# Hybrid encoder layer: block sums' transfers begun from GpSimd, and a delta-rule scan in which the state meets the keys themselves

## The chip, the cores and the metric

One core of a Trainium2 chip. The metric is the device time of one execution in microseconds, the median of several runs. Engines by name: TensorE (PE), VectorE (DVE), ScalarE (ACT), GpSimd (POOL) and SyncE (SP), which only issues DMA transfers here.

## What is computed

One encoder layer on 1024 tokens of width 1024, all in float32. Three mixers run side by side on a projection of the normalised input: a gated delta rule in both directions (4 heads of 128, chunks of 64), attention of 8 heads, and cross-attention of 4 heads into 256 memory tokens. Their outputs are gated and merged; an MLP of width 4096 with squared ReLU follows (`w_up`, `w_down`). The delta rule, cut to what the change touches (one direction, one chunk at a time):

```python
rhs = jnp.concatenate([vb, kb * jnp.exp(gc)[..., None]], axis=-1)
sol = lax.linalg.triangular_solve(lmat, rhs, left_side=True, lower=True, unit_diagonal=True)
u, w = sol[..., :dv], sol[..., dv:]
...
def step(state, inp):
    u_i, w_i, q_i, k_i, a_i, gl = inp
    v_new = u_i - jnp.einsum("bhcd,bhdv->bhcv", w_i, state)
    o = jnp.einsum("bhcd,bhdv->bhcv", q_i, state) + jnp.einsum("bhcs,bhsv->bhcv", a_i, v_new)
    state = state * jnp.exp(gl)[..., None, None] + jnp.einsum("bhcd,bhcv->bhdv", k_i, v_new)
    return state, o
```

With T the inverse of the triangular matrix (beta folded in), u = T·v and w = T·(k·exp(gc)), so v_new = T·v − (T·(k·exp(gc)))·S = T·(v − exp(gc)·(k·S)).

## The kernel before

The layer runs in stages. In the order of the trace: projection, convolution and preparation of keys and queries to about 445 us; the delta-rule scan, 448 to 571 us; the attention stage, 588 to 1018 us; the branch stage with the gated merge, from 1018 us; then the output projection, the MLP's first gemm, and from about 1650 us the second one, by `w_down`.

Large gemms split each float32 operand into a high and a low part (`split`, L138 to L140) and take three products. `ld` (L97) issues a transfer from SP. Tiles come from pools with a few buffers, and an instruction that writes a buffer waits for the last reader of what was in it. Each engine, and each queue, works in the order of its instructions. That order comes from a scheduler that simulates a timeline, except that TensorE's in the attention stage is pinned to the program's.

**The scan** (loop at L870 to L883) has 16 steps. A step takes two chunks at once, one of the forward and one of the backward direction, in the two halves f of the 128 partitions, for 4 heads. `scan_pre(n)` prepares step n and is written ahead of the step before. It loads `tf`/`Tr` (the inverse T), `kn` (keys), `vn` (values), `wq` (queries in the slots 1 and 2 of four) and `Ar`; it transposes half of T (`ca,tf` on TensorE) and copies it (L790). Then `vn·Tr` gives T·v, which ACT copies to `u` (L797). GpSimd makes `ke` (L792) and multiplies `kn` by `eg` = exp(gc) (L799); `Tr·kn` gives w, transposed, and ACT copies it into the slots 0 and 3 of `wq` (L803). `scan_main(n)` is the part that needs the state `St`: `wq·St` (two PSUM tiles `ps_sm`, 4 heads each, which hold both w·S and q·S in different halves), VectorE's subtraction from `u` (L817, one for each half), `ke·u` (8 products), VectorE's update of `St` (L829, 8 operations), ACT's scaling of q·S into `o` (L833, 8 operations), `ar·u`, and the sum into `oacc` (L841). In the second half of the steps `dn_out` (L846) normalises and stores finished chunks, on VectorE, ACT, GpSimd and TensorE.

**The attention stage** (loop at L1043) has 64 steps t. In each, TensorE does the scores of step t + 2, the transposes of step t, and in between pieces of the gate projection and of `cross()`. `cross()` loads keys and values of a head of the cross-attention into `mkv`, a tile with one buffer, four transfers, once for each of 4 heads; so a head's load waits for the products of the head before.

**Block sums.** Each step t also calls `block_sums(t // 4, t % 4)` (L1024 to L1032), 64 calls. One call loads two pieces of `w_down` into a tile `wc` (2 transfers of 128 KB), makes four differences on GpSimd (L1031) and stores the 256 KB tile to `wt_d` in HBM, which only the last gemm reads. The pool of `wc` has 2 buffers; a load into one waits for the store of what was there. All these transfers are issued by SP through `ld`, in one queue with all other loads of the stage (`qh`, `cxq`, `mkv`, `w_raw`) and stores.

Of the kernel before, what the change touches and what calls it, by code (L numbers as in the profile page):

```python
# [9 lines left out]
F32 = mybir.dt.float32  # L10
F32R = mybir.dt.float32r
AF = mybir.ActivationFunctionType
ALU = mybir.AluOpType
# [6 lines left out]
P = 128  # L20
# [43 lines left out]
def bc(ap, axis, n):  # L64
    a = ap.unsqueeze(axis)
    shape = list(a.shape)
    shape[axis] = n
    return a.broadcast_to(shape)
# [18 lines left out]
def hybrid_block(tc, x, mem, mix_norm_w, w_in, dn_conv_w, dn_a_log, dn_dt_bias, dn_norm_w, q_norm_w, k_norm_w,  # L87
                 mem_norm_w, w_mem_kv, w_branch, w_out, ffn_norm_w, w_up, w_down, final_norm_w, ca_d, cb_d, rope_d,
                 out, dbg=None):
    nc = tc.nc  # L90
    pe, act, dve, gp = TensorE(tc), nc.scalar, nc.vector, nc.gpsimd
    def ld(out, in_):
        if out.dtype == F32R:
            out = out.bitcast(F32)
        if in_.dtype == F32R:
            in_ = in_.bitcast(F32)
        return nc.sync.dma_start(out=out, in_=in_)  # L97
# [4 lines left out]
    def pool(st, name, bufs=1, space=None, side=None):  # L102
        kw = {}
        if space is not None:
            kw["space"] = space
        if side is not None:
            kw["side"] = side
        if space is not DRAM:
            kw["reuse_waits"] = "tile"
        return st.enter_context(tc.tile_pool(name=name, bufs=bufs, **kw))  # L110
# [70 lines left out]
    kT_d = dram.tile([8, P, 4, P], F32, name="kT_d")  # L181
# [16 lines left out]
    wt_d = [dram.tile([P, 4, 512], F32, name=f"wt_d{k}") for k in range(16)]  # L198
# [5 lines left out]
    def ps_mm():  # L204
        return pmm.tile([P, 512], F32, name="ps_mm", tag="mm")

    def ps_dn():
        return pp.tile([P, 512], F32, name="ps_dn", tag="dn", bufs=4)
# [22 lines left out]
    eg = cor.tile([P, 2, 8, 4], F32, name="eg")  # L231
# [25 lines left out]
    for c in range(0, D, 512):  # L257
        ps = ps_mm()
# [9 lines left out]
    for m in range(8):  # L268
# [3 lines left out]
        for g in range(2):  # L272
            ps = ps_dn()
# [17 lines left out]
    R = [slice(0, 64), slice(64, 128)]  # L291
# [147 lines left out]
    for h in range(4):  # L439
# [20 lines left out]
        for m in range(8):  # L460
            for f in range(2):
                pe.matmul(psq[f * 64:(f + 1) * 64, 2 * m:2 * m + 2], lhsT=sq[:, m * P + (1 - f) * 64:m * P + (2 - f) * 64],
                          rhs=ones, start=True, stop=True)
# [268 lines left out]
    for j in range(1, 63):  # L732
        n = 63 - j
# [18 lines left out]
    dp = pool(dst, "dp", bufs=2, side="right")  # L752
# [7 lines left out]
    def f4(a):  # L760
        return a.rearrange("p h c -> p (h c)")

    def nps():
        return ps1b.tile([P, 512], F32, name="ps_sm", tag="sm", bufs=4)

    def nps2():
        return ps1b.tile([P, 512], F32, name="ps_sp", tag="sp", bufs=2)

    def scan_pre(n):
        y = 0 if n < 8 else 1  # L770
        m = n if y == 0 else 15 - n
        a = y
        b = 1 - a
        tr, ar = Tr[n % 2], Ar[n % 2]
        ys = slice(y * 4, y * 4 + 4)
        tf = dp.tile([P, 4, 64], F32, name="tf", tag="tf")
        ld(out=tf[R[a]], in_=ts_d[m, a, ys].rearrange("h r c -> r h c"))
        ld(out=tr[R[b], :, R[b]], in_=ts_d[m, b, ys].rearrange("h r c -> r h c"))
        kn = dp.tile([P, 4, P], F32, name="kn", tag="kn")
        vn = dp.tile([P, 4, P], F32, name="vn", tag="vn")  # L780
        wq = dp.tile([P, 4, 4, 64], F32, name="wq", tag="wq")
        ld(out=kn, in_=kn_d[m])
        ld(out=vn, in_=vn_d[m])
        ld(out=wq[:, :, 1:3], in_=qT_d[m].rearrange("p h (f c) -> p h f c", f=2))
        for f in range(2):
            ld(out=ar[R[f], :, R[1 - f]], in_=at_d[m][R[f], ys])
        ps = nps2()
        for h in range(4):
            pe.matmul(ps[R[a], h * 64:(h + 1) * 64], lhsT=tf[R[a], h], rhs=ident[R[a], R[a]], start=True, stop=True)
        act.copy(out=tr[R[a], :, R[a]], in_=ps[R[a], :256].rearrange("p (h c) -> p h c", h=4))  # L790
        ke = dp.tile([P, 4, P], F32, name="ke", tag="ke")
        gp.tensor_tensor(out=ke, in0=kn, in1=bc(kd[:, y, m], 2, P), op=ALU.mult)  # L792
        u = dp.tile([P, 4, P], F32, name="u", tag="u")
        ps = nps2()
        for h in range(4):
            pe.matmul(ps[:, h * P:(h + 1) * P], lhsT=tr[:, h], rhs=vn[:, h], start=True, stop=True)
        act.copy(out=f4(u), in_=ps)  # L797
        if n > 0:
            gp.tensor_tensor(out=kn, in0=kn, in1=bc(eg[:, y, m], 2, P), op=ALU.mult)  # L799
            ps = nps2()  # L800
            for h in range(4):
                pe.matmul(ps[:, h * P:(h + 1) * P], lhsT=kn[:, h], rhs=tr[:, h], start=True, stop=True)
            act.copy(out=wq[:, :, 0::3], in_=ps.rearrange("p (h f c) -> p h f c", h=4, f=2))  # L803
        return y, m, [y, 1 - y], ar, ke, u, wq

    def scan_main(n, pre):
        y, m, pair, ar, ke, u, wq = pre
        o = dp.tile([P, 4, P], F32, name="o", tag="o")
        pss = []
        if n > 0:  # L810
            for f in range(2):
                ps = nps()
                pss.append(ps)
                for h in range(4):
                    pe.matmul(ps[:, h * P:(h + 1) * P], lhsT=wq[:, h, 2 * f:2 * f + 2].rearrange("p f c -> p (f c)"),
                              rhs=St[pair[f]][:, h], start=True, stop=True)
                dve.tensor_tensor(out=f4(u)[R[f]], in0=f4(u)[R[f]], in1=ps[R[f]], op=ALU.subtract)  # L817
        if n < 15:
            psk = [nps(), nps()]
            for h in range(4):  # L820
                for f in range(2):
                    pe.matmul(psk[f][:, h * P:(h + 1) * P], lhsT=ke[R[f], h], rhs=u[R[f], h], start=True, stop=True)
        for f in range(2 if n < 15 else 0):
            s, ps = St[pair[f]], psk[f]
            if n == 0:
                act.copy(out=f4(s), in_=ps)
            else:
                for h in range(4):
                    dve.scalar_tensor_tensor(out=s[:, h], in0=s[:, h], scalar=el[f][:, y, m, h:h + 1],  # L829
                                             in1=ps[:, h * P:(h + 1) * P], op0=ALU.mult, op1=ALU.add)  # L830
        for f, ps in enumerate(pss):
            for h in range(4):
                act.activation(out=o[R[1 - f], h], in_=ps[R[1 - f], h * P:(h + 1) * P], func=AF.Copy,  # L833
                               scale=egs[R[1 - f], y, m, h:h + 1])
        ps = nps()
        for h in range(4):
            scan_end[0] = pe.matmul(ps[:, h * P:(h + 1) * P], lhsT=ar[:, h], rhs=u[:, h], start=True, stop=True)
        if n == 0:
            act.copy(out=f4(oacc[m]), in_=ps)
        elif y == 0:  # L840
            dve.tensor_tensor(out=f4(oacc[m]), in0=f4(o), in1=ps, op=ALU.add)  # L841
        else:
            dve.tensor_tensor(out=f4(o), in0=f4(o), in1=ps, op=ALU.add)
            gp.tensor_tensor(out=oacc[m], in0=oacc[m], in1=o, op=ALU.add)
# [24 lines left out]

    scan_end = [None]  # L870
    pre = scan_pre(0)
    for n in range(16):
        nxt = scan_pre(n + 1) if n < 15 else None
        scan_main(n, pre)
        pre = nxt
        if n == 4:
            tc.keep_in_program_order(ld(out=kA, in_=ka_d))
        if n == 5:
            tc.keep_in_program_order(ld(out=kB, in_=kb_d))
        if n > 9:  # L880
            dn_out(17 - n)
# [142 lines left out]
    def block_sums(k, c):  # L1024
        cs = slice(c * P, (c + 1) * P)
        w = wcp.tile([P, 4, P], F32, name="wc", tag="wc")
        for j in range(2):
            src = w_down[(2 * k + j) * P:(2 * k + j + 1) * P].rearrange("p (h c) -> p h c", h=2)
            ld(out=w[:, 2 * j:2 * j + 2], in_=src[:, :, cs])
        for o, a, b in ((0, 1, 0), (1, 3, 1), (3, 3, 0), (2, 2, 3)):  # L1030
            gp.tensor_tensor(out=w[:, o], in0=w[:, a], in1=w[:, b], op=ALU.subtract)  # L1031
        ld(out=wt_d[k][:, :, cs], in_=w)  # L1032

    cr = cross()
    fill(24 * GATES[0])
# [7 lines left out]
    for t in range(NT):  # L1043
        if t + 2 < NT:
            q_scores(t + 2)
        if t % 2 == 0 and t:
            q_out(t // 2 - 1)
        next(cr, None)
        fill(FILL[0])
        q_trans(t, 0)  # L1050
        block_sums(t // 4, t % 4)
        fill(FILL[1])
        q_trans(t, 1)
        fill(FILL[2])
# [19 lines left out]
    def ps2():  # L1074
        return pq.tile([P, 512], F32, name="ps2", tag="ps2")
# [11 lines left out]
    for bi, b in enumerate(order):  # L1087
# [7 lines left out]
        for mt in range(8):  # L1095
# [11 lines left out]
            for f in range(2):  # L1107
                c = slice(f * 512, (f + 1) * 512)
# [35 lines left out]
    for m in range(8):  # L1144
# [5 lines left out]
        for f in range(2):  # L1150
            c = slice(f * 512, (f + 1) * 512)
            ps = ps2()
# [192 lines left out]
    for name in ("P1", "P2", "P6", "P7", "P4", "P5", "P3"):  # L1345
        ps = [ps2() if m < 3 else ps_mm() for m in range(4)]
        for kg in range(16 // KG):
# [9 lines left out]
            for m in range(4):  # L1357
# [7 lines left out]
                u, o1, o2 = us[m], o[m], o[m + 4]  # L1365
# [61 lines left out]
```

## Time and profile before

| | |
|---|---|
| median of 3 runs | 1926.17 us (1922.19 to 1927.29) |
| profiled execution: its own time, span | 1923.72 us, 1921.9 us |
| TensorE busy, mean granted clock | 1827.6 us (95%), 0.977 |
| VectorE, ACT, GpSimd busy | 1237.4, 808.2, 532.4 us |
| chain of work that ended last | TensorE 82%, DMA 8%, VectorE 5%, GpSimd 2% |
| data moved | 313.28 MB, 163 GB/s on the mean |

The profile is of one execution. Times in rows are microseconds from the start of the span; "granted clock" is the share of TensorE's full clock that the chip allowed. A row of a timeline groups like instructions that follow each other; a wait is put down to the semaphore that came last.

### The profile page before, as it was taken

Reading aid. Unit: us, or ns where it says so; the run is one execution under the profiler, and the core shown is the slowest. Engines: PE = TensorE matmul, PEld = TensorE weight load, DVE = VectorE, ACT = ScalarE, POOL = GpSimd, SP = SyncE. Lnnn points to the kernel's source line nnn. Section 1 sums busy time; section 2 is a strip of 40 time slices with the busy share of each in tenths; the row PEclk is TensorE's granted clock in tenths of the full one; section 3 lists DMA queues with packets and bytes.
Section 4 is the critical chain, followed back from the end, with each engine's and each line's share of the span. In section 5 each row is a group of like instructions: output and inputs, shape, how many; then the busy total and the mean of one; then the engine's idle time right before and its main releaser. Section 6 shows DMA issues by size and latency. Waiting matters only on the chain.

```text
span 1921.9 us, 27229 instructions
## 1 busy us (share of the span) xinstructions
PE 1827.6 (95%) x9891; PEld 1546.2 (80%) x9891; DVE 1237.4 (64%) x1795; ACT 808.2 (42%) x1597; POOL 532.4 (28%) x598
## 2 busy tenths in 40 slices
PE   6999999999999959869999999989999999999998
PEld 5888788988988848758888887867888888788886
DVE  4677989993676636646663456367787776555562
ACT  5453434653545636546663113133222223543341
POOL 1003131231343434442000052123656561011300
PEclk8999999998999979979999999999999999999999
DMA  7235664566656565564215545412454449666662
GB/s 152 71 106 165 196 200 138 160 181 187 186 150 197 167 187 171 179 190 146 88 55 167 201 150 183 135 66 80 147 179 142 159 174 350 240 206 201 203 198 66
DMA packets 340313, 313.28 MB, mean 163 GB/s; under 512 B 51986, under 2 KB 271314, under 8 KB 339667
## 3 DMA queue, kind: packets, MB, share of 16 engines
q1 hardware_dynamic: 339858, 311.02, 51.8%
q8 instruction: 78, 1.28, 0.3%
q10 hardware_dynamic: 320, 0.52, 0.1%
q14 instruction: 57, 0.46, 0.1%
HBM read 208.15 MB, written 103.32 MB: 162 GB/s over the span
## 4 chain that ended last, share of the span: by engine, by line
PE 82%; DMA 8%; DVE 5%; POOL 2%; issue 2%; ACT 1%; SPq 1%; POOLq 0%; ACTq 0%; DVEq 0%
PE ps L81 34%; PE ps_mm L81 30%; PE ps_dn L81 4%; PE ps_t L84 3%; PE ps_sm L81 3%; PE ps_t L81 2%; PE ps_s L81 2%; DMA wc<-in_w_down_dram 2%; PE ps_sp L81 2%; DMA wt_d<-wc 2%; SPq L97 1%; POOL wc L1031 1%; DMA xs_d<-dd 1%; DMA X<-xs_d 1%; DVE c_acc L412 1%
## 5 line engine op out<-in xcount | busy, mean ns | idle before, releaser
L81 PE MATMUL ps<-hs,ws 128*128 128x512 f32 x1344 | 312.6, 392 | 0.3 <-ACT hs L139 0.2
L81 PEld LDWEIGHTS ps<-hs,ws 128*128 128x128 f32 x1344 | 251.7, 189 | 52.0 <-ACT hs L139 0.8
L81 PE MATMUL ps_mm<-hTh,w_hi 128*128 128x512 f32 x704 | 286.6, 407 | 5.4 <-ACT hTh L139 4.8
L81 PE MATMUL ps_mm<-hTl,w_hi 128*128 128x512 f32 x704 | 284.4, 404 | 0.0
L81 PE MATMUL ps_mm<-hTh,w_lo 128*128 128x512 f32 x704 | 278.2, 395 | 3.1 <-DVE w_lo L140 3.1
L140 DVE TENSOR_TENSOR ab_lo<-ab_raw,ab_hi 128x1024 fp32r<-128x1024 f32 x112 | 139.7, 1296 | 94.4 <-issue 65.5
L1031 POOL TENSOR_TENSOR wc<-wc 128x128 f32<-128x128 f32 x256 | 127.7, 508 | 182.6 <-DMA wc<-in_w_down_dram 172.6
L139 ACT CAST ab_hi<-ab_raw 128x1024 fp32r<-128x1024 f32 x112 | 111.7, 1050 | 142.7 <-PE ps_mm L81 89.0
L81 PEld LDWEIGHTS ps_mm<-hTh,w_hi 128*128 128x128 f32 x704 | 134.3, 191 | 30.1 <-ACT hTh L139 5.0
L81 PEld LDWEIGHTS ps_mm<-hTh,w_lo 128*128 128x128 f32 x704 | 133.9, 190 | 29.1 <-DVE w_lo L140 3.3
L81 PEld LDWEIGHTS ps_mm<-hTl,w_hi 128*128 128x128 f32 x704 | 134.3, 191 | 20.8
L81 PE MATMUL ps<-ab_hi 128*128 128x512 f32 x336 | 129.9, 389 | 1.6 <-ACT ab_hi L139 1.6
L81 PE MATMUL ps<-ab_lo,ab_hi 128*128 128x512 f32 x336 | 130.6, 389 | 0.1
L81 PE MATMUL ps<-ab_hi,ab_lo 128*128 128x512 f32 x336 | 130.6, 389 | 0.0
L140 DVE TENSOR_TENSOR ptl<-ps_t,pth 128x512 fp32r<-128x512 f32 x128 | 86.5, 687 | 60.2 <-ACT pth L139 59.9
L139 ACT CAST w_hi<-w_raw 128x1024 fp32r<-128x1024 f32 x64 | 67.3, 1052 | 117.3 <-PE ps_mm L81 107.1
L140 DVE TENSOR_TENSOR w_lo<-w_raw,w_hi 128x1024 fp32r<-128x1024 f32 x64 | 83.0, 1298 | 41.6 <-ACT w_hi L139 40.7
L1116 POOL TENSOR_TENSOR g_acc<-g_acc,g_l 128x512 f32<-128x512 f32 x28 | 41.4, 1482 | 246.0 <-ACT g_yh L139 211.9
L139 ACT CAST pth<-ps_t 128x512 fp32r<-128x512 f32 x128 | 74.2, 586 | 51.1 <-PE ps_t L84 50.9
L901 DVE TENSOR_REDUCE nmx<-ps_s 128x1 f32<-128x1024 f32 x64 | 78.2, 1222 | 17.9 <-PE ps_s L81 17.0
L902 ACT ACTIVATE pm<-ps_s,nmx 128x1024 f32<-128x1024 f32 x64 | 71.7, 1120 | 41.1 <-DVE nmx L901 41.1
L84 PEld LDWEIGHTS ps_t<-ca,pm 128*128 128x128 f32 x512 | 64.1, 142 | 18.6 <-DVE cpl L140 1.4
(325 smaller groups left out, 4080.9 us busy)
## 6 DMA issues: line engine op xcount, KB each, us to landing
w_raw<-in_w_in_dram SPq DMA_DIRECT2D x50, 512.0 KB
ab_raw<-ab_d SPq DMA_DIRECT2D x96, 256.0 KB
w_raw<-in_w_up_dram SPq DMA_DIRECT2D x34, 512.0 KB
wc<-in_w_down_dram SPq DMA_DIRECT2D x128, 128.0 KB
wt_d<-wc SPq DMA_DIRECT2D x64, 256.0 KB
ab_d<-f_a SPq DMA_DIRECT2D x32, 512.0 KB
ab_raw<-wt_d SPq DMA_DIRECT2D x64, 256.0 KB
g_d<-gt SPq DMA_DIRECT2D x48, 256.0 KB
```

Source lines behind the costliest of these rows:

```text
L81: return self._put(self.tc.nc.tensor.matmul(*a, **k))
L84: return self._put(self.tc.nc.tensor.transpose(*a, **k))
L97: return nc.sync.dma_start(out=out, in_=in_)
L139: act.copy(out=hi, in_=src)
L140: (eng or dve).tensor_tensor(out=lo, in0=src, in1=hi.bitcast(F32), op=ALU.subtract)
L412: dve.scalar_tensor_tensor(out=acc[:, o], in0=xn[:, i], scalar=cw[:, ct, j:j + 1], in1=acc[:, o], op0=ALU.mult, op1=ALU.add)
L901: dve.tensor_reduce(out=nmx, in_=ps, axis=AX.X, op=ALU.max, negate=True)
L902: act.activation(out=p_out, in_=ps, func=AF.Exp, bias=nmx, accum_out=sm)
L1031: gp.tensor_tensor(out=w[:, o], in0=w[:, a], in1=w[:, b], op=ALU.subtract)
L1116: (dve if bi == 2 and mt > 5 else gp).tensor_tensor(out=acc[mt][:, c], in0=acc[mt][:, c], in1=t, op=ALU.add)
```

## The change

Two parts. The block sums' loads and stores are issued by GpSimd (`gp.dma_start`) and no longer by SP. In the scan, T is applied once: the keys are loaded, transposed, straight into the slots 0 and 3 of `wq`, so `wq·St` gives k·S; VectorE makes exp(gc)·(k·S) − v in place in `vn` (8 operations of 64 × 128 for a step); only then comes `vn·Tr`, and ACT's `u`, with scale −1 (L817 of the changed kernel). `Tr·kn`, its copy, the multiply of `kn` by `eg` and the two subtractions are gone.

```diff
@@ scan_pre
         ld(out=wq[:, :, 1:3], in_=qT_d[m].rearrange("p h (f c) -> p h f c", f=2))
+        if n > 0:
+            for f in range(2):
+                ld(out=wq[:, :, 3 * f], in_=kT_d[m][:, :, R[f]])
...
-        u = dp.tile([P, 4, P], F32, name="u", tag="u")
-        ps = nps2()
-        for h in range(4):
-            pe.matmul(ps[:, h * P:(h + 1) * P], lhsT=tr[:, h], rhs=vn[:, h], start=True, stop=True)
-        act.copy(out=f4(u), in_=ps)
-        if n > 0:
-            gp.tensor_tensor(out=kn, in0=kn, in1=bc(eg[:, y, m], 2, P), op=ALU.mult)
-            ps = nps2()
-            for h in range(4):
-                pe.matmul(ps[:, h * P:(h + 1) * P], lhsT=kn[:, h], rhs=tr[:, h], start=True, stop=True)
-            act.copy(out=wq[:, :, 0::3], in_=ps.rearrange("p (h f c) -> p h f c", h=4, f=2))
-        return y, m, [y, 1 - y], ar, ke, u, wq
+        return y, m, [y, 1 - y], ar, ke, vn, wq, tr
@@ scan_main, after the products wq·St of half f
-                dve.tensor_tensor(out=f4(u)[R[f]], in0=f4(u)[R[f]], in1=ps[R[f]], op=ALU.subtract)
+                for h in range(4):
+                    dve.scalar_tensor_tensor(out=vn[R[f], h], in0=ps[R[f], h * P:(h + 1) * P], scalar=eg[R[f], y, m, h:h + 1],
+                                             in1=vn[R[f], h], op0=ALU.mult, op1=ALU.subtract)
+
+        u = dp.tile([P, 4, P], F32, name="u", tag="u")
+        ps = nps2()
+        for h in range(4):
+            pe.matmul(ps[:, h * P:(h + 1) * P], lhsT=tr[:, h], rhs=vn[:, h], start=True, stop=True)
+        act.activation(out=f4(u), in_=ps, func=AF.Copy, scale=-1.0 if n > 0 else 1.0)
@@ block_sums
-            ld(out=w[:, 2 * j:2 * j + 2], in_=src[:, :, cs])
+            gp.dma_start(out=w[:, 2 * j:2 * j + 2], in_=src[:, :, cs])
...
-        ld(out=wt_d[k][:, :, cs], in_=w)
+        gp.dma_start(out=wt_d[k][:, :, cs], in_=w)
```

The order of TensorE's instructions in one step of the first half of the scan, before (a number behind a name tells apart the two buffers of a tile):

```order
L81 MATMUL ps_sp<-ca,tf 64x64 x4
L81 MATMUL ps_sm<-St_4604,wq 128x128 x4
L81 MATMUL ps_sm<-St_4605,wq 128x128 x4
L81 MATMUL ps_sp<-vn,Tr_4607 128x128 x4
L81 MATMUL ps_sp<-Tr_4607,kn 128x128 x4
L81 MATMUL ps_sm<-u,ke 128x128 x8
L81 MATMUL ps_sm<-u,Ar_4608 128x128 x4
```

and now:

```order
L81 MATMUL ps_sm<-St_4604,wq 128x128 x4
L81 MATMUL ps_sm<-St_4605,wq 128x128 x4
L81 MATMUL ps_sp<-vn,Tr_4606 128x128
L81 MATMUL ps_sp<-ca,tf 64x64 x4
L81 MATMUL ps_sp<-vn,Tr_4606 128x128 x3
L81 MATMUL ps_sm<-u,ke 128x128 x8
L81 MATMUL ps_sm<-u,Ar_4608 128x128 x4
```

Before, `vn·Tr` and `Tr·kn` between `wq·St` and `ke·u` belong to the next step; now `vn·Tr` there belongs to the same step. ACT's order in such steps of the changed kernel (L793 copies the next step's half of T):

```order
L833 ACTIVATE o<-ps_sm,egs 64x128 x8
L817 ACTIVATE u<-ps_sp 128x512
L793 COPY Tr_4607<-ps_sp 64x4x64
L833 ACTIVATE o<-ps_sm,egs 64x128 x8
L817 ACTIVATE u<-ps_sp 128x512
L793 COPY Tr_4606<-ps_sp 64x4x64
```

The copy to `u` stands behind all eight scalings of `o`. SP's queue ahead of the second load of `mkv` in the attention stage, before:

```order
L97 DMA wc<-in_w_down_dram 128x2x128
L97 DMA wt_d_204<-wc 512x1x128
L97 DMA wc<-in_w_down_dram 128x2x128 x3
L97 DMA wt_d_205<-wc 512x1x128
L97 DMA g_d_0_93<-gt 128x512
L97 DMA wc<-in_w_down_dram 128x2x128
L97 DMA w_raw<-in_w_in_dram 128x8x128
L97 DMA mkv<-mk_d 128x256
```

and now:

```order
L97 DMA g_d_0_93<-gt 128x512
L97 DMA y_d_125<-yt 128x256
L97 DMA qh<-qs_d 128x2x256
L97 DMA g_d_0_93<-gt 128x512
L97 DMA w_raw<-in_w_in_dram 128x8x128
L97 DMA mkv<-mk_d 128x256
```

No transfer of block sums stands in SP's queue any more; they stand in GpSimd's, between its subtractions:

```order
L1029 DMA wc<-in_w_down_dram 128x2x128 x4
L1031 TENSOR_TENSOR wc<-wc 128x128 x8
L1032 DMA wt_d_200<-wc 512x1x128 x2
L1029 DMA wc<-in_w_down_dram 128x2x128 x4
L1031 TENSOR_TENSOR wc<-wc 128x128 x7
L1032 DMA wt_d_201<-wc 512x1x128
```

So four loads, eight subtractions and two stores follow one another for each pair of blocks, and the next pair's loads stand behind the stores.

## Rows read from the trace of the kernel before

**Rows 1.** Page, part 1: busy us (share of the span) x instructions.
```profile
PE 1827.6 (95%) x9891; PEld 1546.2 (80%) x9891; DVE 1237.4 (64%) x1795; ACT 808.2 (42%) x1597; POOL 532.4 (28%) x598
```

**Rows 2.** Attention stage by stretch: length, busy us (x), PEclk, DMA share, GB/s.
```profile
588.18:690.20 102.02, 102.02 (x584) 87.09 (x583) 70.27 (x110) 68.99 (x122) 45.47 (x88) 1.00 0.61 183
690.20:712.00 21.80, 2.34 (x18) 2.06 (x17) 1.52 (x2) 1.72 (x4) 7.70 (x17) 0.66 0.65 198
712.00:718.60 6.60, 6.56 (x23) 5.33 (x24) 2.88 (x7) 2.92 (x7) 2.41 (x5) 0.57 0.57 174
```

**Rows 3.** Waits of TensorE, 572 to 1031 us: sum, times, longest.
```profile
PE ps_mm L81 <- DMA mkv<-mk_d: 41.2, 2, 21.7
```

**Rows 4.** Waits of the SP queue, 600 to 900 us.
```profile
SPq L97 <- POOL wc L1031: 73.6, 48, 3.8
SPq L97 <- DMA wt_d<-wc: 52.1, 37, 3.2
```

**Rows 5.** Timeline of SP: start, duration, operation.
```profile
707.43 0.58 SPq L97 DMA_DIRECT2D mkv<-mk_d  x1
```

**Rows 6.** Timeline of TensorE, idle time before it in brackets.
```profile
712.04 1.99 PE L81 MATMUL ps_mm<-mkv,cxq 128*128 128x256 f32 x6 [19.50 <-DMA mkv<-mk_d]
```

**Rows 7.** Timeline of SP, third reload of `mkv`.
```profile
920.16 0.32 SPq L97 DMA_DIRECT2D mkv<-mk_d  x1
```

**Rows 8.** Timeline of SP, a store and the next load of block sums.
```profile
877.39 0.57 SPq L97 DMA_DIRECT2D wt_d<-wc  x1
...
879.89 3.20 SPq L97 DMA_DIRECT2D wc<-in_w_down_dram  x4
```

**Rows 9.** Timeline of GpSimd: the last block sums, the branch stage's first operation.
```profile
882.85 2.44 POOL L1031 TENSOR_TENSOR wc<-wc 128x128 f32<-128x128 f32 x5 [4.52 <-DMA wc<-in_w_down_dram]
...
1099.02 2.33 POOL L1116 TENSOR_TENSOR g_acc<-g_acc,g_l 128x512 f32<-128x512 f32 x1 [211.88 <-ACT g_yh L139]
```

**Rows 10.** Timeline of TensorE in the scan: first, steady and last step.
```profile
456.34 1.91 PE L81 MATMUL ps_sp<-vn,Tr 128*128 128x128 f32 x8
...
474.42 2.05 PE L81 MATMUL ps_sm<-St,wq 128*128 128x128 f32 x16
476.31 1.06 PE L81 MATMUL ps_sp<-vn,Tr 128*128 128x128 f32 x8
477.20 1.06 PE L81 MATMUL ps_sp<-Tr,kn 128*128 128x128 f32 x8
478.19 1.71 PE L81 MATMUL ps_sm<-u,ke 64*128 64x128 f32 x16
479.83 1.16 PE L81 MATMUL ps_sm<-u,Ar 128*128 128x128 f32 x8
...
481.52 2.05 PE L81 MATMUL ps_sm<-St,wq 128*128 128x128 f32 x16
...
566.87 2.05 PE L81 MATMUL ps_sm<-St,wq 128*128 128x128 f32 x16 [0.24 <-ACT wq L803]
```

**Rows 11.** Timeline of VectorE in one scan step.
```profile
475.61 0.68 DVE L817 TENSOR_TENSOR u<-u,ps_sm 64x512 f32<-64x512 f32 x1 [0.58 <-PE ps_sm L81]
...
479.38 2.16 DVE L829 SCALAR_TENSOR_TENSOR St<-St,el,ps_sm 128x128 f32<-128x128 f32 x8 [2.18 <-PE ps_sm L81]
```

**Rows 12.** ACT by line, 467 to 510 us: busy, mean ns, idle before, releaser.
```profile
L833 ACT ACTIVATE o<-ps_sm,egs 64x128 f32<-64x128 f32 x48 | 14.2, 358 | 8.8 <-DVE u L817 8.6
...
L797 ACT COPY u<-ps_sp 128x512 f32<-128x512 f32 x6 | 3.4, 570 | 0.0
```

**Rows 13.** Other stretches, columns as in rows 2.
```profile
460.22:516.48 56.26, 56.26 (x515) 52.82 (x513) 31.83 (x86) 28.99 (x89) 15.99 (x16) 1.00 0.66 193
...
536.80:543.60 6.80, 6.80 (x36) 6.25 (x35) 5.03 (x15) 2.00 (x7) 4.59 (x4) 0.50 0.60 164
...
1299.00:1312.00 13.00, 9.06 (x54) 6.25 (x53) 9.82 (x22) 7.08 (x20) 5.77 (x4) 1.00 0.23 64
```

**Rows 14.** Timeline of TensorE in a late scan step.
```profile
535.92 2.67 PE L81 MATMUL ps_sm<-u,ke 64*128 64x128 f32 x16 [1.53 <-DVE u L817]
```

More of the change, by code (lines that the diff above doesn't have):

```diff
@@ L792, in scan_pre @@
         gp.tensor_tensor(out=ke, in0=kn, in1=bc(kd[:, y, m], 2, P), op=ALU.mult)
-        u = dp.tile([P, 4, P], F32, name="u", tag="u")
-        ps = nps2()
-        for h in range(4):
-            pe.matmul(ps[:, h * P:(h + 1) * P], lhsT=tr[:, h], rhs=vn[:, h], start=True, stop=True)
-        act.copy(out=f4(u), in_=ps)
-        if n > 0:
-            gp.tensor_tensor(out=kn, in0=kn, in1=bc(eg[:, y, m], 2, P), op=ALU.mult)
-            ps = nps2()
-            for h in range(4):
-                pe.matmul(ps[:, h * P:(h + 1) * P], lhsT=kn[:, h], rhs=tr[:, h], start=True, stop=True)
-            act.copy(out=wq[:, :, 0::3], in_=ps.rearrange("p (h f c) -> p h f c", h=4, f=2))
-        return y, m, [y, 1 - y], ar, ke, u, wq
+        return y, m, [y, 1 - y], ar, ke, vn, wq, tr
     def scan_main(n, pre):
-        y, m, pair, ar, ke, u, wq = pre
+        y, m, pair, ar, ke, vn, wq, tr = pre
         o = dp.tile([P, 4, P], F32, name="o", tag="o")
```

## The prediction

> **What bounds the kernel now.** I read the busy line first: TensorE works 95% of the span [rows 1], so a gain must come from a stretch where it stands still, and a loss can come wherever its work is put in series with something else. The change touches two stretches: the scan (448 to 571 us) and the attention stage (588 to 1018 us) in which the block sums run.
>
> The table by stretch shows the attention stage: TensorE is busy without a gap up to 690 us, then works only 2.34 of 21.80 us [rows 2]. Its waits name one cause: two waits for `mkv`, 41.2 us in sum [rows 3]. The other queue shows why the load is late. SP waits in program order, and from 600 to 900 us it stood 73.6 us for GpSimd's subtractions on `wc` and 52.1 us for a store of `wt_d` [rows 4]. Those are the waits of block sums, 125.7 us in which nothing behind them could be issued. TensorE ran dry 2 us later, but the load of `mkv` was issued only at 707.43 [rows 5], and the first product on it came at 712.04, after 19.5 us of idleness [rows 6]. The third reload of `mkv`, after the last block sum, was issued at 920.16 [rows 7] and no wait for it is listed: two waits, not three [rows 3].
>
> **Block sums on GpSimd: the gain.** The changed order of SP has no `wc` or `wt_d` row ahead of `mkv`, so the two stalls look like the third reload, at nothing: −41.2 us. What is late next is the `cxq` load behind `mkv`; behind the third reload no wait for it shows, so I put it at 0. Behind the stall TensorE was granted 0.57 of its clock for 6.6 us [rows 2], nearly all of it the lower of its two levels (1.2 in place of 2.4 GHz), which loses 6.6 × 0.43 = 2.8 us; two stalls give −5.7. Sum **−46.9**. The bounds are 0 (the load late in any case) and −46.9; I take the whole, since the third reload is the nearest row.
>
> Here a rule speaks against the change. By the rows, 125.7 us of SP's time went into waiting, and what was lost at 690 us was an issue that came late. The Trainium skill (DMA: Bandwidth & Descriptors, section on issuing engines not being separate DMA queues) says that transfers started by any engine run on the same 16 DMA engines, and that starting them elsewhere saves only the sequencer's time to start them, usually small. By that rule the sum would have 0 in place of −46.9. The trace agrees that the DMA engines are shared, but a wait ahead of the issue is more than the issue itself.
>
> **What the move costs on GpSimd.** Its in-order queue now holds, for a pair of blocks, 4 load issues, 8 subtractions and 2 store issues, and the next loads into a buffer wait for its store. The rows give the steps: store issued 877.39, next load 879.89 [rows 8], so 2.5; first subtraction 882.85 [rows 9], so 3.0; five subtractions in 2.44, so 2.0 for the four ahead of the first store. One pair takes about 7.4 us plus five issues (4 loads and 1 store). What an issue costs GpSimd no row shows. From below I bound it by SP's 0.57 [rows 8], from above by the 3.0 us in which a whole load is issued and lands. I take 1.1, twice SP's price, nearer the lower row as that is an issue and the upper one also holds the transfer. Then a pair is 12.9 us and 32 pairs 413 us: begun near 585 they end near 998. Nothing else stands in that queue until the branch stage, whose first GpSimd operation starts at 1099.02 [rows 9], about 40 us earlier in the changed kernel, so at 1060. `wt_d` is read only in the last stage. So this costs 0 up to 15 us for a pair, that is 1.5 us for an issue. At the lower bound they end near 910; at 3.0 they end near 1300, some 240 us late.
>
> **The scan: the loss.** In a step TensorE runs `wq·St` at 474.42, `vn·Tr` 476.31, `Tr·kn` 477.20, `ke·u` 478.19, `ar·u` 479.83 and the next step's `wq·St` at 481.52 [rows 10]: 7.10 us with no gap, because the two products with `Tr` need no state and cover VectorE's subtraction. The change removes `Tr·kn` (0.9 us of TensorE), its ACT copy, GpSimd's multiply by `eg` and the two subtractions of VectorE. It adds eight small VectorE operations and two 128 KB loads for a step, and puts `vn·Tr` and ACT's `u` behind the state. Steps, from the start of `wq·St` (t = 0):
> - VectorE: its state update starts 1.19 after `ke·u` and takes 2.16 for 8 operations, 0.27 each [rows 10, 11]; with `oacc`'s sum behind it (as wide as a subtraction, 0.68) VectorE comes free at t = 1.3. A new operation lies between 0.17 (a fourth of the subtraction, 0.68 [rows 11]) and that 0.27; I take 0.27, the same operation: first half ready at 2.4, second at 3.45.
> - ACT: in the changed order all eight `o` stand ahead of `u`. They take 14.2/48 = 0.30 each [rows 12] and, as in the trace now, wait for VectorE's read of the same PSUM tile: 2.4 to 3.6 and 3.6 to 4.8. Then `u`, 0.57 (3.4/6): 5.35.
> - TensorE: `wq·St` to 2.0, `vn·Tr` done near 4.3, then idle until `ke·u` at 5.4; `ke·u` and `ar·u` take 2.73. The step is 8.1 us.
>
> Steps 1 to 8 took 56.3 us, 460.22 to 516.48 [rows 13]; at 8.1 they take 65: +8.7. Steps 9 to 14 took 50.4, up to 566.87 [rows 10]; there VectorE also has the output work, so I take 8.9 for a step, 53.4: +3. The last step is longer by ACT's wait, +2.5. At the start `vn·Tr` and `Tr·kn` of step 1 stand ahead of its `wq·St`, from 456.34 [rows 10] to 460.22, and go: 3.9 less half an `ar·u` that stays, −3.5. Sum +10.7, rounded to **+10**. The 256 KB of new loads stand a step ahead of their use: from below 0, from above their bytes at that stretch's 193 GB/s [rows 13], 1.4 us for a step, 20 in all; I take 0, since the DMA share there is 0.66.
>
> **The clock.** Each step now has gaps of about 0.7 and 1.2 us. Rows disagree on what such gaps do: after one of 1.53 us at 534.4 `ke·u` took 2.67 in place of 1.71 [rows 14], and the clock stood at 0.50 for 6.8 us [rows 13]; between 1299 and 1312, with TensorE busy 9.06 of 13 us, it stayed at 1.00 [rows 13]. Lower end 0. Upper end: in a step at the lower level `ke·u` and `ar·u` take 2.7 us more and `wq·St` 1 more, so 12 in place of 8; half of each step at that level is 2 × 15, or 28 us. As the busy share (6.2 of 8.1) is that of the second row I take the nearer end with two or three falls of 3 us: **+8**.
>
> **Sum.** Against the profiled execution, 1923.7: −46.9 + 10 + 8 = 1895. The median of the three runs is 2.4 above that execution, so I state **1896**.
>
> **Rivals.**
> - *The clock holds in the scan.* For it: the stretch at 1299. Against: the fall at 534. Then 1923.7 − 46.9 + 10 = 1887. Chance 0.25.
> - *The clock falls in nearly every step*: 1887 + 28 = 1915. For and against are the same rows, turned round. Chance 0.17.
> - *GpSimd's queue overruns.* If an issue costs 2.0, a pair takes 17.4 and the block sums end at 585 + 557 = 1142, 82 us after the branch stage wants GpSimd. The price is those 82 less what TensorE can do ahead of it, so 1895 + 72 = 1967, slower. It decides at 1.5 us for an issue (1.8 for a time slower than now). For it: issues need GpSimd itself now, and VectorE is busy beside it in this stage (70 of 102 us [rows 2]). Against: over 90 us of slack at SP's price. In the Trainium skill (SBUF — State Buffer, the trap named "DVE blocks DMA") GpSimd writes the descriptors of its own transfers and is locked out while VectorE runs certain operations on two ports; no run here shows it yet. Chance 0.12.
> - *The stalls stay*, since the shared DMA engines (share 0.65 while TensorE stood still [rows 2]) make `mkv` late: 1923.7 + 18 = 1942, slower; it is also the case by the first rule above. Against: the load landed 4.6 us after its issue at that very share [rows 5, 6]. Chance 0.04.
>
> **How the numbers follow.** My forecast (a few falls of the clock) has the remaining 0.42. The range 1878 to 1917 takes in the holding clock with 9 us for a cheaper start or shorter steps, and the clock that falls throughout; it leaves out the two slow rivals and a little more, 0.2 in all. About 0.3% (5.8 us) is what a measurement of this kernel can tell from no change; faster by that is under 1920. Faster: 0.25 + 0.17 + 0.42 = 0.84, less 0.03 for a clock rival that runs past 1920: 0.81. Same 0.05, slower 0.14.
>
> **What would show it.** Right: no wait of TensorE for `mkv`, `mkv` issued within 1 us of its buffer coming free; scan steps of 8 us with two gaps, one ended by ACT's `u`; block sums ending near 1000; GpSimd's first branch operation waiting for its inputs, not for its queue. Wrong: scan steps of 10 us or more, TensorE waiting in the scan for `wq`'s loads, a new wait of TensorE for the branch's sums after 1050, or block sums that still run past 1070.

## The result, and the profile after

| | before | changed |
|---|---|---|
| median of 4 runs each | 1926.6 us | 1906.32 us (1904.97 to 1909.09) |
| ratio, 95% interval | | 0.9901 [0.9882, 0.9921] |
| profiled execution, span | 1923.72, 1921.9 us | 1909.09, 1907.3 us |
| scan, first `ca,tf` to the end of the last `ar·u` | 122.2 us | 148.6 us |
| end of the scan to GpSimd's first branch operation | 528.2 us | 481.6 us |

By the medians the kernel is 20 us faster. Between the two profiled executions there are two large terms of opposite sign: the attention stage gives back 46.6 us (528.2 − 481.6) and the scan costs 26.4 (148.6 − 122.2). These two executions are only 14.6 us apart, the changed kernel's being the slowest of its four; the other 5.6 us lie ahead of the scan (1.5) and behind GpSimd's first branch operation (4.1, and there the granted clock from 1241 to 1321 us is 0.89, where it was 0.96 in the like stretch before, 1260 to 1340). Of the 4.1, `e1` below has 3.4 and `e2` 0.1, so they seem to come with the block sums' move; no run tests why.

Of the busy line ([rows 1] before) GpSimd's figure is the new one: its issues now count as its work.

```profile
PE 1822.3 (96%) x9771; PEld 1539.3 (81%) x9771; DVE 1254.8 (66%) x1885; ACT 799.1 (42%) x1582; POOL 653.4 (34%) x775
```

**Attention stage.** TensorE's timeline, and then SP's, at the place of [rows 5, 6]. The last product of a head reads `mkv` at 709.19; the reload is issued at 709.61, as that product ends (709.19 + 0.39), and the next head's first product comes at 720.47, 10.9 us after the issue. It waits for nothing (no idle time in brackets).

```profile
709.19 0.39 PE L81 MATMUL ps_mm<-cph,mkv 128*128 128x512 f32 x1
...
720.47 0.88 PE L81 MATMUL ps_mm<-mkv,cxq 128*128 128x256 f32 x6
```

```profile
709.61 0.32 SPq L97 DMA_DIRECT2D mkv<-mk_d  x1
```

SP still waits a lot, for ACT's gate tiles above all, but TensorE does not wait for anything that stands behind it (waits of SP from 600 to 900 us, as in [rows 4]; no row of `wc` or `wt_d` is left):

```profile
SPq L97 <- ACT gt L721: 151.9, 27, 8.4
```

The stretch of the scan and the one behind it, columns as in [rows 2]: the scan at a granted clock of 0.84, then 481.6 us in which TensorE is busy for 481.56, at 1.00.

```profile
450.00:598.70 148.70, 114.56 (x888) 103.40 (x889) 86.79 (x279) 53.39 (x162) 30.47 (x28) 0.84 0.58 159
...
598.70:1080.30 481.60, 481.56 (x2691) 410.89 (x2691) 303.10 (x462) 278.32 (x486) 264.88 (x450) 1.00 0.53 173
```

**GpSimd's queue** by line, 600 to 990 us (busy, mean ns of one, idle before, releaser): a load's issue takes 0.73 us, a store's 0.755. Then its timeline at the end of the block sums, as in [rows 9]: they end at 984, and the branch stage finds GpSimd idle for 96.7 us.

```profile
L1029 POOL DMA_DIRECT2D wc<-in_w_down_dram x128 | 92.5, 728 | 69.5 <-DMA wt_d<-wc 66.3 <-issue 2.7
L1032 POOL DMA_DIRECT2D wt_d<-wc x64 | 47.2, 755 | 5.2 <-POOL wc L1031 3.9 <-issue 1.3
```

```profile
982.13 1.50 POOL L1032 DMA_DIRECT2D wt_d<-wc  x2
1080.31 2.35 POOL L1116 TENSOR_TENSOR g_acc<-g_acc,g_l 128x512 f32<-128x512 f32 x1 [96.69 <-ACT g_yh L139]
```

**The scan.** One step on TensorE, VectorE and ACT, as in [rows 10, 11]. After `ke·u` at 474.97 VectorE runs 8 updates of `St` (476.14), the sum of `oacc` (478.21) and 8 `vn` (478.81) back to back; TensorE waits 1.35 us for them, does one head of `vn·Tr`, the next step's `ca,tf`, the other heads, and waits 0.84 us for ACT's `u` (482.42). In this step the clock then falls: `ke·u` takes 2.08 us, not 1.16.

```profile
477.06 1.95 PE L81 MATMUL ps_sm<-St,wq 128*128 128x128 f32 x16
480.36 0.49 PE L81 MATMUL ps_sp<-vn,Tr 128*128 128x128 f32 x2 [1.35 <-DVE vn L810]
480.78 0.68 PE L81 MATMUL ps_sp<-ca,tf 64*64 64x64 f32 x8
481.38 0.94 PE L81 MATMUL ps_sp<-vn,Tr 128*128 128x128 f32 x6
483.16 2.08 PE L81 MATMUL ps_sm<-u,ke 64*128 64x128 f32 x16 [0.84 <-ACT u L817]
485.17 1.70 PE L81 MATMUL ps_sm<-u,Ar 128*128 128x128 f32 x8
486.70 1.95 PE L81 MATMUL ps_sm<-St,wq 128*128 128x128 f32 x16
```

```profile
476.14 2.16 DVE L829 SCALAR_TENSOR_TENSOR St<-St,el,ps_sm 128x128 f32<-128x128 f32 x8 [3.20 <-PE ps_sm L81]
478.21 0.68 DVE L841 TENSOR_TENSOR oacc<-o,ps_sm 128x512 f32<-128x512 f32 x1
478.81 2.31 DVE L810 SCALAR_TENSOR_TENSOR vn<-ps_sm,eg,vn 64x128 f32<-64x128 f32 x8
```

```profile
480.03 2.30 ACT L833 ACTIVATE o<-ps_sm,egs 64x128 f32<-64x128 f32 x8 [4.96 <-DVE vn L810]
482.42 0.60 ACT L817 ACTIVATE u<-ps_sp 128x512 f32<-128x512 f32 x1
```

TensorE's waits in the scan (445 to 600 us: sum, times, longest), 22.5 us for VectorE's `vn` and ACT's `u`; before (449 to 571 us, first line) 2.0 were for VectorE's `u`:

```profile
PE ps_sm L81 <- DVE u L817: 2.0, 2, 1.5
```

```profile
PE ps_sp L81 <- DVE vn L810: 11.7, 11, 1.4
PE ps_sm L81 <- ACT u L817: 10.8, 12, 1.3
```

From one start of `wq·St` to the next a step takes 8.2 us when the clock stays (468.81 to 477.06) and 9.6 when it falls (477.06 to 486.70); the step behind such a fall is shorter, 7.6 (to 494.34), as TensorE then waits 0.80 us for VectorE and not 1.35. `ke·u` is long, 1.88 or 2.08, in 7 of the 14 steps 1 to 14.

### The profile page after: what moved, and what is told of

Same layout as the page of the kernel before. It is cut to its first block, busy times and chain, and to the rows that moved or that the text cites. A ratio compares the mean times of both kernels' runs of the same rounds, so it can differ in the third digit from the quotient of the medians.

```text
span 1907.3 us, 27016 instructions
## 1 busy us (share of the span) xinstructions
PE 1822.3 (96%) x9771; PEld 1539.3 (81%) x9771; DVE 1254.8 (66%) x1885; ACT 799.1 (42%) x1582; POOL 653.4 (34%) x775
## 4 chain that ended last, share of the span: by engine, by line
PE 84%; DVE 7%; DMA 3%; ACT 3%; issue 2%; SPq 0%; POOL 0%; ACTq 0%; POOLq 0%; DVEq 0%
PE ps_mm L81 33%; PE ps L81 33%; PE ps_t L84 4%; PE ps_dn L81 3%; PE ps_t L81 3%; PE ps_s L81 3%; PE ps_sm L81 2%; ACT o L833 1%; DVE St L829 1%; DVE vn L810 1%; DMA w_raw<-in_w_out_dram 1%; PE ps_sp L81 1%; PE ps_mm L84 1%; DVE c_acc L412 1%; DMA w_raw<-in_w_mem_kv_dram 1%
## 5 line engine op out<-in xcount | busy, mean ns | idle before, releaser
L139 ACT CAST ab_hi<-ab_raw 128x1024 fp32r<-128x1024 f32 x112 | 111.7, 1050 | 143.8 <-PE ps_mm L81 81.6
L140 DVE TENSOR_TENSOR ptl<-ps_t,pth 128x512 fp32r<-128x512 f32 x128 | 86.5, 687 | 58.3 <-ACT pth L139 57.9
L1029 POOL DMA_DIRECT2D wc<-in_w_down_dram x128 | 92.5, 728 | 69.5 <-DMA wt_d<-wc 66.3
L1116 POOL TENSOR_TENSOR g_acc<-g_acc,g_l 128x512 f32<-128x512 f32 x28 | 41.4, 1482 | 131.2 <-ACT g_yh L139 96.7
## 6 DMA issues: line engine op xcount, KB each, us to landing
wc<-in_w_down_dram POOLq DMA_DIRECT2D x128, 128.0 KB, 2.9
```

The costliest lines, as they stand in the source:

```text
L139: act.copy(out=hi, in_=src)
L140: (eng or dve).tensor_tensor(out=lo, in0=src, in1=hi.bitcast(F32), op=ALU.subtract)
L1029: gp.dma_start(out=w[:, 2 * j:2 * j + 2], in_=src[:, :, cs])
L1116: (dve if bi == 2 and mt > 5 else gp).tensor_tensor(out=acc[mt][:, c], in0=acc[mt][:, c], in1=t, op=ALU.add)
```

## The experiments

### Each part alone

`e1_sums_only`: the kernel before, with the two hunks of `block_sums`. `e2_scan_only`: the changed kernel without them.

```diff
 e1 (against before)
-            ld(out=w[:, 2 * j:2 * j + 2], in_=src[:, :, cs])
+            gp.dma_start(out=w[:, 2 * j:2 * j + 2], in_=src[:, :, cs])
-        ld(out=wt_d[k][:, :, cs], in_=w)
+        gp.dma_start(out=wt_d[k][:, :, cs], in_=w)
```

> The kernel before with only the block sums' transfers begun from GpSimd; the scan as before. Theory (SP's in-order queue held the load of mkv back): both waits of TensorE for mkv, 41.2 us, are gone with the low clock behind them, 1926.6 - 46.9 = 1880 us, and the scan keeps its 122 us. Rival (the 16 shared DMA engines made mkv late, whoever issues): the waits stay, 1926 us. Second rival (the scan's length depends on the block sums): the scan is 140 us or more here too.

> The changed kernel with the block sums' transfers given back to SP: the scan's change alone. Theory (the two parts add up, the scan loses 26.5 us): 1926.6 + 26.5 = 1953 us, scan 148 us, the two waits for mkv back at about 41 us. Rival (the scan's loss comes from its own extra loads colliding with GpSimd's transfers): scan near 130 us, 1934 us.

Block sums alone: 1876.64 us against 1925.53 of the kernel before on the same chip, ratio 0.9743 [0.9715, 0.9772]. No wait for `mkv` is listed. The scan alone: 1947.69 us, ratio 1.0123 [1.009, 1.0156], with the waits for `mkv` back and the scan's two waits beside them (11.7 us for `vn`, 11.6 for `u`). Stretch of the scan in `e1` (columns as in [rows 2]), then TensorE's wait for `mkv` in `e2`, 449 to 1050 us:

```profile
448.50:567.20 118.70, 115.69 (x1009) 107.97 (x1010) 73.22 (x186) 60.11 (x173) 45.23 (x41) 0.96 0.60 171
```

```profile
PE ps_mm L81 <- DMA mkv<-mk_d: 38.4, 3, 22.0
```

−49 and +22 us add up to −27, the changed kernel's −20 within the intervals' width. Of the difference 3.4 us can be named: in `e1` the old scan is shorter too, 118.7 us where it was 122.2, as its one long step takes 9.1 us and not 12.5. The new scan takes 148.6 us with block sums on GpSimd and 148.2 with them on SP, so its loss does not hang on them.

By the Trainium skill (DMA: Bandwidth & Descriptors, section on issuing engines not being separate DMA queues) transfers started by any engine run on the same 16 DMA engines. The trace agrees: from 600 to 985 us of the changed kernel GpSimd's transfers take 25.5% of the 16 engines' time and those from SP 26.7%. The same section of the Trainium skill says that starting transfers on several engines saves only the time to start them. Here the measurement differs, and it decides: `e1` gained 49 us. An issue that waits for a semaphore held back all that stood behind it in SP's queue, 125.7 us in all [rows 4]. `e1` beats both kernels.

### Is it the waits in SP's queue?

Two halves of the move: `e3_stores_only` gives GpSimd the stores alone, `e8_loads_only` the loads alone (each one of the two lines of the diff above).

> The kernel before with only the 64 stores of block sums begun from GpSimd; the 128 loads stay on SP. Theory (what holds mkv back is that SP's queue stands at a semaphore of the block sums' cycle, whatever instruction it stands at): SP no longer waits for GpSimd's subtractions, but its loads then wait for the same store, 110 us or more in all; TensorE still waits over 30 us for mkv and the time is 1915 to 1927 us. Rival (the gain comes in shares, from each wait or issue taken off SP): the 73.6 of 125.7 us of waits are gone, TensorE's wait is about 17 us, 1900 us.

> The kernel before with only the 128 loads of block sums begun from GpSimd; the 64 stores stay on SP. Theory: SP stands at the stores until GpSimd's subtractions are done, which now wait for loads that GpSimd itself issues; only half the waits' places are left in the queue, so TensorE's wait for mkv stays but may shrink: 10 to 41 us, 1885 to 1926 us. Rival (issues, not waits, made mkv late): two thirds of the issues are gone, wait about 14 us, 1895 us.

One execution each: 1912.4 us (2.6 below the forecast range) and 1920.5 (within it), against 1923.8 of before beside them. Neither half gives its share of the 47 us. Waits of SP, 560 to 990 us, and of TensorE, 570 to 1050 us, first of `e3`, then of `e8`:

```profile
SPq L97 <- DMA wt_d<-wc: 179.6, 55, 6.9
```
```profile
PE ps_mm L81 <- DMA mkv<-mk_d: 31.0, 3, 17.0
```

```profile
SPq L97 <- DMA wc<-in_w_down_dram: 135.6, 32, 6.3
SPq L97 <- POOL wc L1031: 133.7, 44, 6.7
```
```profile
PE ps_mm L81 <- DMA mkv<-mk_d: 35.9, 4, 16.3
```

SP stands longer at the block sums' semaphores than before (as in [rows 4], 76.8 + 52.6 = 129 us in this window): 180 us at one place, 269 at two. Taking one kind of transfer off the queue moves the wait to the other kind, since both belong to one cycle of load, difference, store and next load. TensorE still waits 31 and 36 us for `mkv`. `e8` takes two thirds of the issues off SP (128 of 192) and leaves 35.9 of 41.2 us, so the number of issues is not the cause. One thing no run separates: in each of these kernels the scheduler also puts SP's other loads in a new order, which in `e9` below costs 10 us.

### The clock in the scan

`e4_filled`: the changed kernel with work added in the two gaps, products that nothing reads; the tile is overwritten by the real ones.

```diff
         u = dp.tile([P, 4, P], F32, name="u", tag="u")
         ps = nps2()
+        if n > 0:
+            with tc.issue_after(last.ins):
+                pe.matmul(ps, lhsT=ident, rhs=f4(ke), start=True, stop=True)
...
             psk = [nps(), nps()]
+            if n > 0:
+                with tc.issue_after(last.ins):
+                    pe.matmul(psk[0][:, :384], lhsT=ident, rhs=f4(ke)[:, :384], start=True, stop=True)
```

> The changed kernel with work added: in each scan step TensorE computes two products that nothing reads (512 and 384 columns, ahead of vn.Tr and ahead of ke.u), placed in the two gaps; the output is the same. Theory (about 10 us of the scan's loss is TensorE's clock, which falls behind the gaps): granted clock of the scan 0.97 or more, no ke.u of 2 us, scan 138 us in place of 148.6, total 1896 us, though there is more work. Rival (the loss is the longer chain alone and the low clock only stretches what is waited for anyway): scan 148 us or longer, 1906 to 1910 us.

1894.2 us (1893.59 to 1896.07), ratio 0.984 [0.981, 0.9871]; changed kernel 0.9901 [0.9882, 0.9921], each against the kernel before measured beside it. More work, 12 us less time. The stretch of the scan, 135.0 us at a granted clock of 0.96 (low only in step 0), and one step:

```profile
447.90:582.90 135.00, 120.17 (x947) 95.50 (x947) 85.40 (x278) 52.48 (x162) 30.46 (x28) 0.96 0.64 175
```

```profile
475.00 1.02 PE L81 MATMUL ps_sp<-ke,ca 128*128 128x512 f32 x2
475.95 0.68 PE L81 MATMUL ps_sp<-ca,tf 64*64 64x64 f32 x8
476.56 1.28 PE L81 MATMUL ps_sp<-vn,Tr 128*128 128x128 f32 x8
477.68 0.81 PE L81 MATMUL ps_sm<-ke,ca 128*128 128x384 f32 x2
479.05 1.16 PE L81 MATMUL ps_sm<-u,ke 64*128 64x128 f32 x16 [0.56 <-ACT u L820]
...
481.13 1.95 PE L81 MATMUL ps_sm<-St,wq 128*128 128x128 f32 x16
```

No `ke·u` behind step 0 is long any more. A step is 7.92 us, not 8.2; I put the 0.3 down to `ca,tf`, which the scheduler has now put ahead of `vn·Tr`, some 4 us in all. So of the 13.6 us by which the scan is shorter up to about 10 are the clock's. Counted with it are the changed kernel's waits in steps 11 to 13 (1.7 us for `Tr`, 1.7 for `ke`, 2.0 at an issue), which are shorter or absent in `e4`; no run tells them apart from the clock.

### The chain in the scan

Three runs with the operations of the changed kernel in another order. `e5_u_first`: ACT's `u` ahead of the eight `o`. `e11_sum_late`: the sum of `oacc` one step later, behind `vn`. `e7_chain_short`: both, and `ca,tf` behind `vn·Tr`.

```diff
 e5 and e7: o behind u
-        for f, ps in enumerate(pss):
+        with tc.issue_after(ui.ins):
+          for f, ps in enumerate(pss):
...
 e11 and e7: the last step's sum, kept in a list, behind the last vn operation vi
+        if late:
+            with tc.issue_after(vi.ins):
+                late.pop(0)()
...
 e7: the transposes of T behind the last product vn.Tr of the step
+        with tc.issue_after(trl[0].ins) if trl[0] is not None else ExitStack():
+            for h in range(4):
+                pe.matmul(ps[R[a], h * 64:(h + 1) * 64], lhsT=tf[R[a], h], rhs=ident[R[a], R[a]], start=True, stop=True)
```

> The changed kernel with one thing reordered: ACT's copy to u ahead of the eight scalings of o. The prediction priced the wait of u behind o at about 1 us of a step. Theory A (as predicted, u stands behind o): ke.u comes 0.5 to 1 us earlier after vn.Tr, a step of 7.3 to 7.7 us at full clock, 1895 us. Theory B (vn.Tr, with the transposes in its middle, is done only when ACT is free anyway): a step stays at 8.2 us and the gap ahead of ke.u at 0.8 us, 1903 to 1909 us.

> The changed kernel with one thing reordered: VectorE's sum of oacc comes one step later, behind the vn operations. Theory (VectorE's 8 state updates, the sum and the 8 vn operations are one chain that sets the step): 0.6 us less for each step at full clock, 7.6 us, TensorE's gap ahead of vn.Tr 0.75 us in place of 1.35, and fewer falls of the clock behind it; scan 130 to 140 us in place of 148, 1890 to 1898 us. Rival (the sum lies beside TensorE's work): no change, 1906 us.

> The changed kernel with the same operations in another order in the scan: ACT's copy to u ahead of the eight scalings of o, VectorE's sum of oacc one step later and behind the vn operations, the transposes of T behind vn.Tr and no longer in its middle. Theory (the step is bound by the chain of VectorE's 8 + 1 + 8 operations, vn.Tr and ACT): 0.6 us from the sum and 0.6 to 0.9 from the transposes and o leave the chain, a step of 6.9 us in place of 8.2, scan 121 to 126 us, total 1879 to 1885 us. Rival (the chain's order is not what sets the step; the lower clock is, and it stays as gaps stay): steps above 8 us, 1900 to 1906 us.

`e5`, one execution: 1916.9 us (1920.0 before beside it), above both forecasts. It gains nothing, and by this one execution it loses: the output work needs `o`, which now comes later, and TensorE waits 10.6 us for `oacc` up to the end of the scan where it waited 0.6. In a step, on TensorE and on ACT, the gap ahead of `ke·u` is the same 0.84 us though `u` now stands first: `u` waits for `vn·Tr`.

```profile
490.40 1.16 PE L81 MATMUL ps_sm<-u,ke 64*128 64x128 f32 x16 [0.84 <-ACT u L817]
```

```profile
489.65 0.60 ACT L817 ACTIVATE u<-ps_sp 128x512 f32<-128x512 f32 x1 [5.04 <-PE ps_sp L81]
```

Step 10 of the changed kernel shows the other half. There `ca,tf` does not stand in the middle of `vn·Tr`, which ends at 543.10; `o` ends at 543.77, `u` comes as `o` ends, and TensorE waits 1.29 us. So `ca,tf` and `o` each hold `u` back, and taking away one alone gains little.

```profile
541.80 1.30 PE L81 MATMUL ps_sp<-vn,Tr 128*128 128x128 f32 x8 [1.35 <-DVE vn L810]
544.39 2.08 PE L81 MATMUL ps_sm<-u,ke 64*128 64x128 f32 x16 [1.29 <-ACT u L817]
```

```profile
541.47 2.30 ACT L833 ACTIVATE o<-ps_sm,egs 64x128 f32<-64x128 f32 x8 [4.81 <-DVE vn L810]
543.67 0.58 ACT L817 ACTIVATE u<-ps_sp 128x512 f32<-128x512 f32 x1
```

`e11`, one execution: 1898.8 us, 0.8 above its forecast; the scan takes 132.6 us. The step is 7.59 us (474.21 to 481.80) where it was 8.2, and the gap ahead of `vn·Tr` 0.76 where it was 1.35: the sum stood in the chain with its whole 0.6 us. The clock falls in 4 of the steps 1 to 14 where it fell in 7.

```profile
474.21 1.95 PE L81 MATMUL ps_sm<-St,wq 128*128 128x128 f32 x16
476.92 0.49 PE L81 MATMUL ps_sp<-vn,Tr 128*128 128x128 f32 x2 [0.76 <-DVE vn L810]
...
479.72 1.16 PE L81 MATMUL ps_sm<-u,ke 64*128 64x128 f32 x16 [0.84 <-ACT u L820]
...
481.80 1.95 PE L81 MATMUL ps_sm<-St,wq 128*128 128x128 f32 x16
```

`e7`: 1885.35 us (1882.2 to 1888.29), ratio 0.9791 [0.9763, 0.9819]. Steps 2 to 6 take 7.10 us each, with gaps of 0.71 and 0.23, and up to step 10 the clock does not fall once; the scan is 126 us.

```profile
481.05 2.05 PE L81 MATMUL ps_sm<-St,wq 128*128 128x128 f32 x16
483.81 1.30 PE L81 MATMUL ps_sp<-vn,Tr 128*128 128x128 f32 x8 [0.71 <-DVE vn L811]
485.04 0.68 PE L81 MATMUL ps_sp<-ca,tf 64*64 64x64 f32 x8
485.95 1.25 PE L81 MATMUL ps_sm<-u,ke 64*128 64x128 f32 x16 [0.23 <-ACT u L821]
...
488.15 2.05 PE L81 MATMUL ps_sm<-St,wq 128*128 128x128 f32 x16
```

It reaches the old step's 7.10, not the 6.9 of the forecast: VectorE's 8 + 8 operations, `vn·Tr`, `u` and `ke·u` still follow one another. I read them as the chain that is left; no run cuts it further. In the second half, with VectorE's output work, steps are 7.1 to 8.2 and one, where the clock falls, 12.7; and `e1` with the old scan stays 9 us ahead.

### How much room GpSimd's queue has

`e1` with every load cut into two (`e9_issues_x2`) and four (`e10_issues_x4`) transfers; `e10`'s edit, of which `e9` has the outer loop alone:

```diff
-            gp.dma_start(out=w[:, 2 * j:2 * j + 2], in_=src[:, :, cs])
+            for i in range(2):
+                for r in (slice(0, 64), slice(64, 128)):
+                    gp.dma_start(out=w[r, 2 * j + i], in_=src[r, i, cs])
```

> Block sums on GpSimd with the scan of before, and every load cut into two transfers of half the size: 8 load issues for a pair of blocks. Theory (a pair's period is the sum of GpSimd's issues at 0.72 us and the transfers' latencies, all hidden until the branch stage wants GpSimd near 1049 us): period 11.8 + 4 x 0.72 = 14.7 us, block sums end near 1050 us in place of 959, time unchanged, 1874 to 1880 us. Rival (more transfers cost time by themselves, through the shared DMA engines): 1885 us or more.

> The same with every load cut into four transfers: 16 load issues for a pair. Theory: period 11.8 + 12 x 0.72 = 20.4 us, block sums end near 1234 us, GpSimd's first operation of the branch stage comes 185 us late and TensorE stands still for most of it: 2030 to 2065 us. Rival (an issue costs GpSimd less for a smaller transfer, or TensorE runs ahead without GpSimd): block sums end before 1100 us, under 1930 us.

`e9`, one execution: 1889.0 us, 12 more than `e1`, and not by the block sums: they end at 994 (forecast 1050), as an issue of half the size takes 0.55 us. TensorE waits 10 us for the first tiles of the branch stage, whose loads the scheduler has put later in SP's order (first one issued at 1001, at 966 in `e1`). The run does not test what it was meant to. `e10`, one execution: 1963.4 us, between its two forecasts. The same wait (10.7 us), and the queue's overrun: issues of 0.58, 17.2 us for a pair where 20.4 were forecast, block sums to 1133, and TensorE stands still for 57.9 us. GpSimd's timeline at the end of the block sums, and TensorE's wait, 1000 to 1200 us:

```profile
1119.91 8.32 POOL L1031 DMA_DIRECT2D wc<-in_w_down_dram  x16 [1.31 <-DMA wt_d<-wc]
...
1131.87 1.46 POOL L1034 DMA_DIRECT2D wt_d<-wc  x2
1133.19 5.07 POOL L1118 TENSOR_TENSOR g_acc<-g_acc,g_l 128x512 f32<-128x512 f32 x4
```

```profile
PE ps_mm L81 <- DVE g_l L1117: 57.9, 1, 57.9
```

The branch operation starts right behind the last store: GpSimd's order is what it waited for. This is the prediction's slow rival (17.4 us for a pair, 1967 us); in the changed kernel GpSimd's queue has 96 us to spare.

## Why the prediction held, and where it was off

- **The time**: 1896 us forecast, in a range from 1878 to 1917, and 1906.3 measured. Most of the 10 us between them is the scan's, whose loss was sized too small by 8.
- **The gain, −46.9 forecast**: −46.6 measured between the end of the scan and the branch stage, −49 by `e1` as a whole, of which 3.4 are the old scan's. The step from [rows 5 to 7] was right: both waits went, the low clock behind them went, and the third reload was the right model for the other two.
- **GpSimd's issues**: taken at 1.1 us, 0.73 measured; a pair 12.9 forecast, 11.9 measured (380 us for 32 pairs, 604 to 984). The end near 998 came at 984 in spite of a later start. The bound from below was nearer than the middle.
- **The scan, +10 forecast at full clock, +8 for the clock**: +26.4 measured. The direction was right, the size too small by 8. A step's length was right (8.1 forecast, 8.2 measured), and so was the chain that sets it, counted from one `ke·u` to the next (474.97 to 483.16): VectorE is done with `vn` after 6.15 us (3.45 + 2.73 forecast), ACT with `o` after 7.36 (7.53) and with `u` after 8.05 (8.08). Missed was a second path of the same length: *"in the changed order all eight `o` stand ahead of `u`"* is true, but `vn·Tr`, with `ca,tf` in its middle, ends when the last `o` does (482.32 and 482.33), so taking `o` away gained nothing (`e5`). The gaps were forecast at about 0.7 and 1.2 us and came out at 1.35 and 0.84. The prediction took 2.73 us for `ke·u` and `ar·u` from [rows 10], where `ke·u` takes 1.71; in the changed kernel it takes 1.16 and the two 2.09 (474.97 to 477.06). So `wq·St` starts 0.64 us earlier and waits that much longer for the same chain of VectorE.
- **Mis-sized terms of the scan**: the end (forecast +2.5, the time from the last `wq·St` to the end of the scan grew from 3.9 to 10.2 us, +6.3, as the output work of VectorE now stands in the chain), the start (−3.5 forecast; 11.6 us before and 10.4 now, −1.2, as TensorE waits 1.4 us for the second `tf`), and the rest, steps 1 to 14, (+11.7 and the clock's +8 forecast, 19.7 together; 106.7 us before, 128.0 now, +21.3). Three late steps took more than 10 us (10.25, 11.11 and 10.47), which the prediction had named as a sign of being wrong.
- **The clock**: I took two or three falls of 3 us, 8 in all; there were seven, and one such fall made its step 1.4 us longer (8.2 to 9.6), up to 10 in all by `e4`. That the term came out near is luck: the falls were more than twice as many and cost about half. The row at 1299 [rows 13] was the wrong one to be nearest to.
- **The rivals**: a clock that holds (`e4` gives what it would be worth) and a clock that falls in every step were both off; half the steps fell. The queue's overrun did not happen, with 96 us to spare. That `mkv` stays late is excluded by `e1`.

What stays open: what decides in which steps the clock falls. Gaps of 0.71 and 0.23 us kept it in five steps in a row (`e7`, steps 2 to 6); gaps of 1.35 and 0.84 lost it in about every second step. One longer gap does not decide it either: behind one of 1.53 us the clock fell in the kernel before [rows 14], behind one of 1.56 it stayed (`e7`, step 8: granted clock 1.00 from 509.9 to 517.8 us).

## What to carry to other kernels

A queue that waits in order is worth reading from its waits, not from its issues: a transfer that is part of a cycle (load, compute, store, reload) should not share a queue with loads that TensorE needs on time, and moving half of the cycle gained little here (11 and 3 us of 49, in one execution each). Before an operation is taken out of a scan by putting another into its serial chain, write down the chain with every operation that stands ahead on the same engines; here 0.9 us of TensorE's work went, and with it the cover of a wait that had cost nothing. And test the parts of a change apart: one was worth 49 us, the other cost 22.

## What the runs showed of the hardware that was not expected

- Added work made a kernel faster: two unread products in each step, about 1.6 us of TensorE, kept the granted clock of the scan at 0.96 in place of 0.84 and took 12 us off the whole.
- GpSimd's issue of a transfer grew far less than its size (eight times the bytes, a quarter more time): a median of 0.74 us for a store of 256 KB, 0.72 for a load of 128 KB, 0.55 for 64 KB (`e9`) and 0.58 for 32 KB on half the partitions (`e10`), with VectorE busy for 63% of the time in the changed kernel's attention stage (303.1 of 481.6 us). The longest issue of a load took 1.07 us in the changed kernel and 1.16 in `e10`. A lockout by VectorE, as the Trainium skill describes it (SBUF — State Buffer, the trap named "DVE blocks DMA"), would have to hide in the 0.3 to 0.6 us by which these stand above their medians; no run here shows more of it.
